# Stores of tiles that ScalarE evicts in the input projection: begun by ScalarE instead of SyncE

## The chip, the core and the metric

The kernel runs on one core of a Trainium2 chip. The time is the device time of one execution in microseconds, as the median of several runs. The core has TensorE (PE in the profile; its weight loads are PEld), VectorE (DVE), ScalarE (ACT), GpSimd (POOL) and SyncE (SP). Each executes its own list of instructions in order. A DMA is an instruction on one of these lists too: its engine waits until the DMA's conditions hold, hands it over to the DMA engines, and goes on. In rows of the profile such instructions carry the name of the engine with a q (SPq, ACTq).

## The reference, cut to what matters

The reference is one inference step of a decoder layer with two kinds of heads on a common input projection: eight heads of attention with forget gates (FoX), and four heads of an mLSTM with a 128 x 128 matrix memory. It handles 2048 new tokens of one prompt and 8 new tokens of each of 8 sampled sequences, which have 8192 past tokens in a paged cache.

```python
z = jnp.einsum('bsd,dc->bsc', x, w_in)          # x: 2048 + 64 tokens of 1024; w_in: 1024 x 3600
fq, fk, fv = z[..., :512], z[..., 512:1024], z[..., 1024:1536]     # attention; fk and fv are outputs
qk_in = z[..., OFF_M_QK:OFF_M_V]                # causal convolution of width 4, silu -> mLSTM q, k
mv = z[..., OFF_M_V:OFF_M_I]
og = jax.nn.sigmoid(z[..., OFF_M_O:] + b_og)    # output gate of the mLSTM
...
mix = jnp.concatenate([fox_h, mn], axis=-1) @ w_o
x1 = _layer_norm(DN_ALPHA * x + mix, ln1_g, ln1_b)
hid = jnp.square(jax.nn.relu(x1 @ w1))
return _layer_norm(DN_ALPHA * x1 + hid @ w2, ln2_g, ln2_b)
```

Keys, values, forget values, the mLSTM's last states and the last inputs of the convolution are outputs as well.

## The kernel before, in words

**Stages.** The work runs in stages: the input projection (up to 988 us of the profile), with the mLSTM beside it; the prompt's attention (to about 1440 us); the output projection with the first norm (to about 1720 us); the MLP with the second norm (the rest). The attention of the sampled sequences over the gathered cache pages runs beside all of them except the prompt's attention. All products of the main stream are exact to f32 by three matmuls on split operands (`mm3`, L137 to L140: high by high, high by low, low by high); ACT makes the high parts (`split_hi`, L130), DVE the low parts (L133).

**Input projection** (`block_a`, L395). It goes through four blocks of 512 prompt tokens (the first has the 64 sampled tokens besides). For each block the columns of w_in are taken in groups of 256: `wload` (L212) has SP load them (tile wra, L220), ACT and DVE split them. In this order the block makes

- mLSTM v, tokens on partitions (`natural`, L399): for each token tile 24 matmuls into a PSUM tile pm, which ACT copies into the SBUF tile st (`stage`, L412, copy L414); st is stored to the scratch dv (L420);
- mLSTM q and k, channels on partitions: ACT copies pm to qi (L447), DVE does the convolution, ACT the tanh (L457), DVE the last factor; stored to the scratch dqk (L459);
- the last rows of the convolution, stored to the outputs conv_sample and conv_prompt (L474, L482);
- the output gate, finished by DVE and stored to dog (L492);
- attention q: ACT scales pm into qst (L513), stored to dq (L514);
- attention k and v, again by copies of L414, stored to the outputs (L527, L532), from which later stages load them.

The PSUM tile pm has four buffers, the SBUF tile st four, wra two.

**mLSTM** (`m_block`, L575). It goes through 16 chunks of 128 tokens, one after another, each in several steps. A chunk loads its q and k (L586, from dqk), v (L589, from dv), two rows of gate values spread over all partitions (Wm, L591, from dM; qa, L593, from dar) and the output gate (og, L637, from dog). ACT takes the exponentials (L596, L598), PE multiplies (L604, L611, L621, L622, L629), ACT scales the result (hh, L573). Then `norm_out` (L544) norms it on DVE and POOL (up to L557), PE transposes it (L561), ACT copies it out of PSUM (ot, L563), and it is stored to the scratch dmix (L564). The tiles qk, Wm, qa, og and ot have one buffer each: the load of the next chunk waits for the last use in this one. `m_sample` (L650) does the same for the sampled sequences, with the state matrices of L707.

**Attention of the sampled sequences** (`sample_attention`, L1184). POOL gathers pages of keys (kraw, L1314) and of values (vt, L1401), two buffers each; DVE transposes the keys (L1316), PE makes the scores (L1327), DVE adds the forget sums (L1334) from tiles which SP loads (L1311); a softmax follows (L1361, L1371), then PE multiplies by the values (L1406).

**Order.** The side streams are cut into steps (`yield`). `tick` (L109) starts a step of the mLSTM for every 2.8 us of planned main-stream products and a step of the sampled attention for every 7.5 us (L21 to L24). From this order of the program a scheduler, which runs when the program is built (L1463), makes the lists of the five engines: it moves instructions against each other where their data permit it, by its own estimate of times. The lists are then fixed.

**Stores before the change.** All stores and loads of the input projection are begun by SP, which takes them in the order of its list. A store on SP waits there until the engine that makes the tile is done with it, and whatever stands behind it in SP's list waits as well. Only L1139 in the MLP has ACT begin loads (tile y).

**Semaphores of the DMAs.** The DMAs that SP and ACT begin take eight semaphores in turn, in the order in which the scheduler places them. Before a DMA is begun, the one before it on the same semaphore must have landed; where this isn't known already from an earlier wait, the list has a wait for it.

Of the kernel before, what the change touches and what calls it, by code (L numbers as in the profile page):

```python
# [19 lines left out]
# microseconds of the main stream's products per step of a side stream  # L20
# [32 lines left out]
def body(ctx, tc, I, O, stages):  # L53
# [3 lines left out]
    # ------------------------------------------------------------------ constants  # L57
# [25 lines left out]
    # pools of the sampled tokens' attention, which runs beside all phases, and of the mLSTM  # L83
# [6 lines left out]
    sqk = []                                         # new k of the sampled tokens  # L90
# [4 lines left out]
    gm = pm.tile([128, 16, 8], F32, name="gm")      # g = i - b and m, tokens on partitions  # L95
# [6 lines left out]
    def beside(gen):  # L102
        """one step of a side stream, whose instructions queue behind the main stream's latest"""
        with ExitStack() as es:
            for i in last.values():
                es.enter_context(tc.issue_after(i.ins))
            return next(gen, 0)

    def tick(us):  # L109
        """keeps the side streams in step with the main one"""  # L110
        macc[0] += us
        while macc[1] and macc[0] > PACE_M:
            macc[0] -= PACE_M
            if beside(macc[1][0]) == 0:
                macc[1].pop(0)
        if not macc[1]:
            macc[0] = 0.0
        acc[0] += us
        while acc[1] is not None and acc[0] > acc[2]:
            acc[0] -= acc[2]  # L120
            if beside(acc[1]) == 0:
                acc[1] = None
# [33 lines left out]
    # ------------------------------------------------------------------ phase A: input projection  # L156
# [16 lines left out]
    # conv weights transposed: [128 ch, 8 groups, 5] with the factor 1/2 of silu(c) = c/2 (1 + tanh(c/2))  # L173
# [38 lines left out]
    def wload(cols):  # L212
        """columns of w_in, [(first, number), ...], in their two parts, for each of the 8 row tiles"""
# [33 lines left out]
    def load_x(bi, tiles):  # L247
        """the block's x with channels on partitions, in two parts; column tiles of two token tiles"""
# [18 lines left out]
    def xcol(bi, t):  # L267
        """column tile and columns of a token tile"""
        blk, pre, off = geom(bi)
        o = off[t]  # L270
        i = int(o >= pre + 256)
        o -= i * (pre + 256)
        return xT[bi][i], slice(o, o + tok_n(t))

    def gate_stream(bi):
# [4 lines left out]
        def gates(z, lg, shape, bb):  # L280
# [16 lines left out]
            # log1p(e) = ln(u) + (e - (u - 1)) / u  # L297
# [21 lines left out]
        def rowset(cols, base, n_el, np_, sample):  # L319
# [32 lines left out]
            # M = m - b (kept in lr), ar = m0 - M, g = i - b  # L352
# [28 lines left out]
            # back to tokens on partitions: g, m  # L381
# [13 lines left out]
    def block_a(bi):  # L395
# [21 lines left out]
        for i in range(2):  # L417
            def sink(t, m, ps, i=i):
                r = tok_r(t)
                SY.dma_start(dv[r:r + m, i * 256:(i + 1) * 256], stage(ps[:, :256], m, 256))  # L420
                if i == 1:
                    V.tensor_copy((gats if t == 16 else gat[:, t])[:, 0:16], ps[:, 256:272])
            natural(sink, (C_V + i * 256, 256), *([(C_FF, 8), (C_I, 8)] if i == 1 else []),
                    hook=None if i else lambda n: load_x(bi, blk[n + 2:n + 3]))
# [3 lines left out]
        # mLSTM q/k, channels on partitions, causal convolution along the free axis  # L428
# [37 lines left out]
        if pre:  # L466
            # conv state of the sampled sequences
# [6 lines left out]
            SY.dma_start(O["conv_sample"].rearrange("l b j c -> (l b j) c"), cs_n)  # L474
        if bi == 3:
# [6 lines left out]
            SY.dma_start(O["conv_prompt"].rearrange("l b j c -> (l b j) c"), ch_n)  # L482
# [12 lines left out]
        # attention q, scaled, channels on partitions; that of the sampled tokens as [channel % 32, sequence, channel // 32, t]  # L495
        for j in range(4):
# [17 lines left out]
            SY.dma_start(dq[j, :, t0:t0 + 512], st)  # L514
            if pre and j % 2 == 1:
                SY.dma_start(dqb[0, :, :, j // 2 * 64:j // 2 * 64 + 64].rearrange("b p c -> p b c"), qr.rearrange("p b i t -> p b (i t)"))
        for i in range(2):
            def sink(t, m, ps, i=i):
# [8 lines left out]
                SY.dma_start(d, st)  # L527
            natural(sink, (512 + i * 256, 256))
        for i in range(2):
            def sink(t, m, ps, i=i):  # L530
                d = v_out(t)[:, i * 256:(i + 1) * 256]
                SY.dma_start(d, stage(ps, m, 256))  # L532
# [5 lines left out]
    # ------------------------------------------------------------------ phase M: mLSTM  # L538
# [5 lines left out]
    def norm_out(hh, np_, og, tok0):  # L544
        """per-head layer norm, output gate, transposed into the mix scratch"""
# [18 lines left out]
        SY.dma_start(dmv[:, 4:8, tok0:tok0 + np_], ot[:, :, :np_])  # L564

    def h_out(pn, h0, den, np_, hh):
        """h = num / max(|nq|, exp(-m)) for the pair of heads in pn"""
# [82 lines left out]
    def m_sample():  # L650
        # the sampled sequences: 8 new tokens each on their own state
# [19 lines left out]
        # keys of the sequence itself only: s >= 8 b  # L671
        for h in range(4):
            G.affine_select(Wv[:, h], Wv[:, h], pattern=[[-8, 8], [0, 8]], compare_op=OP.is_ge, fill=0.0, base=0, channel_multiplier=1)
        # bm[s, b] = 1 where token s belongs to sequence b
# [4 lines left out]
        # w_key[s] = W[s, last token of s's sequence]  # L679
# [25 lines left out]
        for h in range(4):  # L705
# [6 lines left out]
            # inter part, transposed [e, (b t)], and its normaliser row  # L712
# [5 lines left out]
            # n . q for all pairs (token, sequence), own sequence picked below  # L718
# [20 lines left out]
            # state update  # L739
# [47 lines left out]
    # ------------------------------------------------------------------ phase B: prompt attention  # L787
    def phase_b():
# [8 lines left out]
        def bank():  # L797
            """a bank of PSUM, every third time that of the sampled tokens' attention, which rests"""
# [13 lines left out]
        def twice(src, t):  # L812
            """a head's columns of token tiles, side by side with themselves"""
# [5 lines left out]
        def forget_values(z, a, n):  # L819
            """forget sums and values of the keys a .. a + n - 1"""  # L820
# [4 lines left out]
        def keys(z, g):  # L825
            """[k_hi; k_lo] of 512 keys, channels on partitions"""
# [14 lines left out]
        def queries(z, g):  # L841
            """[q_hi; q_hi] and [q_lo; q_lo] of two query tiles"""
# [10 lines left out]
        def scores(z, g):  # L853
            """scores of two query tiles against their causal keys, with -L of the keys and the row maximum"""
# [34 lines left out]
        def values(z, g, sc):  # L889
            """exponentials, row sums, weighted values [channels, queries]"""  # L890
# [8 lines left out]
            # P^T in chunks of four key tiles; even and odd key tiles add up in two column halves  # L899
# [31 lines left out]
        def finish(z, half):  # L931
            """1 / row sums as a row, spread over the head's partitions"""
# [44 lines left out]
    # ------------------------------------------------------------------ phase O: output projection, first norm  # L977
# [6 lines left out]
    def raw():  # L984
        """a slot of the ring for weights on their way in"""
        return pcw.tile([128, 1024], F32, name="wr", bufs=4)

    def landing(n=128):
        """a slot of the ring for activations on their way in"""
# [46 lines left out]
    # ------------------------------------------------------------------ phase C: MLP, second norm  # L1036
    def phase_c():
# [5 lines left out]
        def piece(src):  # L1043
            """a 4 KB piece of a weight matrix in its two parts"""
# [14 lines left out]
        def sampled():  # L1059
            """output projection and first norm of the sampled tokens"""  # L1060
# [22 lines left out]
        def load(ci):  # L1083
            """the block's tokens with channels on partitions, in two parts"""
# [99 lines left out]
def sample_attention(tc, I, O, ps_, pps, cst, ident, sqk, dnl, dR, dmix, dqb):  # L1184
    """FoX attention of the sampled tokens over the gathered pages."""
    nc = tc.nc
    V, A, G, T, SY = nc.vector, nc.scalar, nc.gpsimd, nc.tensor, nc.sync
    # ---- indices
# [7 lines left out]
    V.tensor_scalar(io[:, 0:1], pi, 31, None, op0=OP.bitwise_and)             # p % 32  # L1196
    V.tensor_scalar(io[:, 1:2], pi, 5, None, op0=OP.logical_shift_right)      # p // 32
    V.tensor_scalar(io[:, 2:3], pi, 7, None, op0=OP.bitwise_and)              # q
    V.tensor_scalar(io[:, 3:4], io[:, 0:1], 3, None, op0=OP.logical_shift_right)  # pg within a head's 32 rows
    fo = ps_.tile([128, 8], F32, name="fo")  # L1200
    V.tensor_copy(fo[:, 0:4], io[:, 0:4])
    V.scalar_tensor_tensor(fo[:, 4:5], fo[:, 0:1], 4.0, fo[:, 1:2], op0=OP.mult, op1=OP.add)  # (p%32)*4 + p//32
    V.scalar_tensor_tensor(fo[:, 5:6], fo[:, 1:2], 8.0, fo[:, 2:3], op0=OP.mult, op1=OP.add)  # (p//32)*8 + q
    for f in range(2):
        V.tensor_scalar(fo[:, 6 + f:7 + f], fo[:, 0:1], 2.0, float(f), op0=OP.mult, op1=OP.add)   # (p%32)*2 + half
# [5 lines left out]
    # V tile (unit u, page group g): partition (k, t) holds tokens 4 t .. 4 t + 3 of page 16 g + 4 u + k  # L1211
# [12 lines left out]
    # ---- reverse cumulated forget values of the past, written to the dR scratch as [b, h, page, (t%4, t//4)]  # L1224
    tri = ps_.tile([128, 128], F32, name="tri")
    V.memset(tri, 1.0)
    # lhsT[p', p]: p' > p in the same half
# [26 lines left out]
    # ---- new keys of the own sequence: additive bias [(h4, pg, q), t]  # L1254
# [8 lines left out]
    # ---- new k with channels on partitions, [sequence, channel % 32, channel // 32, t]  # L1263
# [7 lines left out]
    # ---- row (h4, q) selectors for the row sums: sel[k=(h4,pg,q), hg, m=(pair, h4, q)]  # L1271
# [32 lines left out]
    def k_step(b, kt, m):  # L1304
        """a quarter of the key tiles kt, kt + 1, channels on partitions"""
# [12 lines left out]
    def qk_step(b, kt):  # L1318
        """scores of the key tiles kt, kt + 1"""
# [18 lines left out]
    def softmax(b):  # L1338
# [11 lines left out]
        # maximum over a row's four page groups, through 32x32 transposes  # L1350
# [30 lines left out]
    def weights(b, u):  # L1381
        """transposed weights of a unit: [(k, t), hg, t%4, pg, h4, q]"""
# [10 lines left out]
    def pv_step(b, kt, f):  # L1393
        """rows (t % 2, hg, h4, q) against the values of the four heads of hg"""
# [72 lines left out]
```

## Time and profile before

| | |
|---|---|
| time, median of 3 runs | 3497.39 us (3494.44 to 3507.39) |
| span of the profiled execution | 3492.4 us |
| instructions | 59522 |
| clock of TensorE granted, mean over the span | 0.985 |
| DMA traffic | 663.15 MB in 446040 packets, 190 GB/s |
| moved by DMAs that ACT begins (queue q10) | 8.65 MB |

The profile is that of one execution, and its span runs from the first to the last instruction; the page gives no other time for it. An engine counts as busy while it computes; instructions that begin a DMA do not count. A row of waits says which engine stood, at which line, and what ended the wait, with the total, the number of cases and the longest one. In a row of the timeline the number in square brackets is the engine's idle time just before the instruction, with the instruction that ended it. A busy TensorE is not one at its peak, since matmuls overlap.

### The profile page before, as it was taken

Reading aid. Unit: us, or ns where it says so; the run is one execution under the profiler, and the core shown is the slowest. Engines: PE = TensorE matmul, PEld = TensorE weight load, DVE = VectorE, ACT = ScalarE, POOL = GpSimd, SP = SyncE. Lnnn points to the kernel's source line nnn. Section 1 sums busy time; section 2 is a strip of 40 time slices with the busy share of each in tenths; the row PEclk is TensorE's granted clock in tenths of the full one; section 3 lists DMA queues with packets and bytes.
Section 4 is the critical chain, followed back from the end, with each engine's and each line's share of the span. In section 5 each row is a group of like instructions: output and inputs, shape, how many; then the busy total and the mean of one; then the engine's idle time right before and its main releaser. Section 6 shows DMA issues by size and latency. Waiting matters only on the chain.

```text
span 3492.4 us, 59522 instructions
## 1 busy us (share of the span) xinstructions
PE 3354.9 (96%) x22428; PEld 2670.1 (76%) x22428; DVE 2178.9 (62%) x5302; ACT 1366.6 (39%) x2818; POOL 897.4 (26%) x942
## 2 busy tenths in 40 slices
PE   8899899999989999999899999999999999999998
PEld 8898778888866666667567677677677777898887
DVE  6747747657558787655556567666666544654555
ACT  3333323334358888512324243332233333443332
POOL 1013213231322222265332324223324111100000
PEclk9999999999999999999899999999999999999999
DMA  6557777775853232586776767768768555442221
GB/s 198 167 167 223 223 220 237 245 246 174 275 163 86 75 81 57 172 275 215 273 250 197 266 214 262 258 200 271 253 218 296 192 164 176 148 154 73 85 85 64
DMA packets 446040, 663.15 MB, mean 190 GB/s; under 512 B 84604, under 2 KB 333760, under 8 KB 444856
## 3 DMA queue, kind: packets, MB, share of 16 engines
q1 hardware_dynamic: 369064, 380.13, 36.1%
q0 software_dynamic: 74304, 270.57, 22.5%
q10 hardware_dynamic: 2384, 8.65, 0.7%
q8 instruction: 176, 2.88, 0.3%
q14 instruction: 112, 0.92, 0.1%
HBM read 598.01 MB, written 61.22 MB: 189 GB/s over the span
## 4 chain that ended last, share of the span: by engine, by line
PE 69%; DMA 15%; DVE 6%; issue 5%; POOL 3%; ACT 1%; SPq 0%; POOLq 0%; DVEq 0%; ACTq 0%
PE py L138 7%; PE py L140 6%; PE py L139 6%; PE ph L138 6%; PE ph L139 6%; PE ph L140 6%; DMA kraw<-cache_k,idxK 4%; PE po L919 4%; DMA vt<-cache_v,idxV 4%; PE pt L910 4%; PE pm L138 4%; PE pm L139 3%; PE pm L140 3%; PE sO L1406 3%; PE pS L871 2%
## 5 line engine op out<-in xcount | busy, mean ns | idle before, releaser
L1150 DVE TENSOR_TENSOR y<-y,py 128x512 f32<-128x512 f32 (+1 forms) x476 | 319.3, 680 | 251.1 <-PE py L140 246.9
L138 PE MATMUL ph<-x1h,wh 128*128 128x512 f32 (+1 forms) x1280 | 455.5, 356 | 2.4 <-ACT wh L130 2.4
L130 ACT ACTIVATE wh<-wr 128x1024 fp32r<-128x1024 f32 x264 | 273.4, 1057 | 466.0 <-PE py L140 264.0
L139 PE MATMUL ph<-x1l,wh 128*128 128x512 f32 (+1 forms) x1280 | 454.7, 355 | 0.0
L140 PE MATMUL ph<-x1h,wl 128*128 128x512 f32 (+1 forms) x1280 | 453.7, 355 | 0.2 <-DVE wl L133 0.2
L1401 POOL DMA_INDIRECT vt<-cache_v,idxV x256 | 257.9, 1007 | 736.1 <-PE sO L1406 701.2
L1316 DVE STREAM_TRANSPOSE kT<-kraw 128x512 f32<-128x512 f32 x512 | 328.3, 684 | 179.8 <-DMA kraw<-cache_k,idxK 178.4
L138 PE MATMUL py<-wh,hh 128*128 128x512 f32 (+1 forms) x1088 | 431.6, 399 | 1.5 <-DVE y L1148 0.8
L139 PE MATMUL py<-wl,hh 128*128 128x512 f32 (+1 forms) x1088 | 429.6, 395 | 0.7 <-DVE wl L133 0.7
L140 PE MATMUL py<-wh,hl 128*128 128x512 f32 (+1 forms) x1088 | 429.1, 395 | 0.0
L1314 POOL DMA_INDIRECT kraw<-cache_k,idxK x256 | 280.9, 1097 | 571.3 <-DVE kT L1316 439.0
L133 DVE TENSOR_TENSOR wl<-wr,wh 128x1024 fp32r<-128x1024 f32 x264 | 333.2, 1269 | 91.4 <-PE ph L140 25.7
L138 PE MATMUL pm<-whi,xh 128*128 128x256 f32 (+2 forms) x1088 | 320.3, 294 | 7.5 <-DVE st L489 4.8
L139 PE MATMUL pm<-wlo,xh 128*128 128x256 f32 (+2 forms) x1088 | 315.7, 290 | 0.0
L140 PE MATMUL pm<-whi,xl 128*128 128x256 f32 (+2 forms) x1088 | 315.4, 290 | 0.0
L138 PEld LDWEIGHTS ph<-x1h,wh 128*128 128x128 f32 x1280 | 240.9, 188 | 46.5 <-issue 11.1
L140 PEld LDWEIGHTS ph<-x1h,wl 128*128 128x128 f32 x1280 | 240.7, 188 | 42.8 <-issue 11.1
L139 PEld LDWEIGHTS ph<-x1l,wh 128*128 128x128 f32 x1280 | 240.6, 188 | 40.4 <-issue 8.6
L138 PEld LDWEIGHTS py<-wh,hh 128*128 128x128 f32 (+1 forms) x1088 | 201.3, 185 | 62.7 <-issue 18.1
L140 PEld LDWEIGHTS py<-wh,hl 128*128 128x128 f32 (+1 forms) x1088 | 201.3, 185 | 55.5 <-issue 9.9
L139 PEld LDWEIGHTS py<-wl,hh 128*128 128x128 f32 (+1 forms) x1088 | 201.5, 185 | 48.5 <-issue 8.6
L138 PE MATMUL pm<-xh,whi 128*128 128x256 f32 (+1 forms) x768 | 224.7, 293 | 0.8 <-ACT qi L447 0.8
(359 smaller groups left out, 6875.1 us busy)
## 6 DMA issues: line engine op xcount, KB each, us to landing
wr<-w SPq DMA_DIRECT2D x256, 512.0 KB
wra<-w_in SPq DMA_DIRECT2D x112, 512.0 KB
xn<-x_prompt SPq DMA_DIRECT2D x32, 512.0 KB
Rb<-dR SPq DMA_DIRECT2D x128, 128.0 KB
dqk<-th SPq DMA_DIRECT2D x32, 256.0 KB
qk<-dqk SPq DMA_DIRECT2D x16, 512.0 KB
qn<-dq SPq DMA_DIRECT2D x128, 64.0 KB
wr<-w_o SPq DMA_DIRECT2D x16, 512.0 KB
```

The costliest lines, as they stand in the source:

```text
L130: last["ACT"] = A.activation(dst, src, AF.Copy, scale=scale)
L133: r = (eng or V).tensor_tensor(dst, src, hi.bitcast(F32), op=OP.subtract)
L138: T.matmul(ps, wh, xh, start=first, stop=False)
L139: T.matmul(ps, wh, xl, start=False, stop=False)
L140: last["PE"] = T.matmul(ps, wl, xh, start=False, stop=stop)
L910: T.transpose(pt[:, k], sc[i][0][k0 // 4][:, k * 128:(k + 1) * 128], ident)
L919: last["PE"] = T.matmul(po[c:c + 64, q0:], z["vn"][:, k], PT[:, k - k0, q0:], start=(k < 2), stop=(k >= nk - 2), skip_group_check=True)
L1150: V.tensor_tensor(y, y, ps, op=OP.add)
L1314: G.indirect_dma_start(out=kraw, out_offset=None, in_=ck, in_offset=IO(ap=idxK[:, b, kt + k, f:f + 1], axis=0))
L1316: V.transpose(z["kT"][:, k, 2 * f + i].rearrange("p b c -> p (b c)"), kraw[:, i * 512:(i + 1) * 512])
L1401: G.indirect_dma_start(out=vt.rearrange("p f c -> p (f c)"), out_offset=None, in_=cv, in_offset=IO(ap=idxV[:, b, pg * 4 + u, f:f + 1], axi ...
L1406: T.matmul(po[r:r + 32], z["PT"][:, hg, 2 * f + g, pg].rearrange("p h q -> p (h q)"), vt[:, g, hg * 256:(hg + 1) * 256], start=(kt == 0 an ...
```

## The change

Seven calls of `dma_start` go from SyncE (`SY`) to ScalarE (`A`). In each of them ScalarE makes the tile that is stored. The tiles, their buffers and the regions written stay as they are. The stores of tiles that DVE finishes (L459 to dqk, L492 to dog) stay on SyncE, as do all loads. The new file also lacks the comments and docstrings of the old one, with the line numbers kept.

```diff
         for i in range(2):
             def sink(t, m, ps, i=i):
                 r = tok_r(t)
-                SY.dma_start(dv[r:r + m, i * 256:(i + 1) * 256], stage(ps[:, :256], m, 256))
+                A.dma_start(dv[r:r + m, i * 256:(i + 1) * 256], stage(ps[:, :256], m, 256))
...
-            SY.dma_start(O["conv_sample"].rearrange("l b j c -> (l b j) c"), cs_n)
+            A.dma_start(O["conv_sample"].rearrange("l b j c -> (l b j) c"), cs_n)
...
-            SY.dma_start(O["conv_prompt"].rearrange("l b j c -> (l b j) c"), ch_n)
+            A.dma_start(O["conv_prompt"].rearrange("l b j c -> (l b j) c"), ch_n)
...
                 A.activation(st[:, i * 256:i * 256 + 256], ps[:, w - 256:], AF.Copy, scale=0.125)
-            SY.dma_start(dq[j, :, t0:t0 + 512], st)
+            A.dma_start(dq[j, :, t0:t0 + 512], st)
...
                 else:
                     st = stage(ps, m, 256)
-                SY.dma_start(d, st)
+                A.dma_start(d, st)
...
                 d = v_out(t)[:, i * 256:(i + 1) * 256]
-                SY.dma_start(d, stage(ps, m, 256))
+                A.dma_start(d, stage(ps, m, 256))
...
         A.copy(ot[:, :, :np_], po[:, :, :np_])
-        SY.dma_start(dmv[:, 4:8, tok0:tok0 + np_], ot[:, :, :np_])
+        A.dma_start(dmv[:, 4:8, tok0:tok0 + np_], ot[:, :, :np_])
```

In order these are L420, L474, L482, L514, L527, L532 and L564; together 137 DMAs.

## The prediction

> **What bounds the kernel now.** First the head of the page, then the busy time of each engine in stretches: the part in which the seven changed lines run (25 to 988 us), the hand-over to the prompt attention (988 to 1004 us) and the output projection (1440 to 1720 us). The columns are length, then busy us and instructions of PE, PEld, DVE, ACT, POOL, granted clock, share of the DMA engines, GB/s.
>
> ```profile
> span 3492.4 us, 59522 instructions
> PE 3354.9 (96%) x22428; PEld 2670.1 (76%) x22428; DVE 2178.9 (62%) x5302; ACT 1366.6 (39%) x2818; POOL 897.4 (26%) x942
> ...
> 25.00:988.00 963.00, 905.72 (x7600) 829.61 (x7599) 605.33 (x1674) 319.61 (x699) 229.94 (x237) 0.98 0.69 213
> ...
> 988.00:1004.00 16.00, 6.76 (x38) 5.20 (x37) 6.97 (x29) 4.79 (x12) 5.24 (x9) 0.78 0.76 205
> ...
> 1440.00:1720.00 280.00, 258.53 (x1485) 185.15 (x1482) 152.45 (x323) 69.81 (x101) 153.35 (x123) 0.94 0.79 263
> ```
>
> TensorE sets the time: in the changed part it is busy for 905.72 of 963 us, one matmul in 905.72 / 7600 = 0.119 us. What a change that removes no matmul can win there is the 57.3 us in which PE stands, and a little clock (0.98 granted). ACT is busy for a third of it (319.61 us). So the next question is what PE stands for, read from the waits of PE (total us, times, longest), first between 18 and 988 us, then, last row, between 1440 and 1720 us.
>
> ```profile
> PE mm L561 <- POOL hh L557: 9.4, 6, 3.6
> PE mn L629 <- ACT hh L573: 4.8, 4, 2.3
> ...
> PE sT L1371 <- ACT Sn L1361: 4.6, 2, 4.3
> PE sQ L1327 <- DVE kT L1316: 4.3, 3, 3.6
> PE mm L604 <- DMA qk<-dqk: 3.9, 2, 2.8
> PE mm L715 <- DMA C<-state_C: 3.5, 3, 2.0
> ...
> PE sO L1406 <- DMA vt<-cache_v,idxV: 14.3, 8, 5.2
> ```
>
> No row names a load of w_in, and only two name a load that SP begins (qk, C: 7.4 us). The rest belongs to the side streams: steps of the mLSTM (L561, L629) and of the sampled attention (L1371, L1327) which stand at a fixed place in PE's program and are reached before their data is there. Now the queue that loses the stores: SP's own waits up to 1010 us.
>
> ```profile
> SPq L532 <- ACT st L414: 67.8, 28, 6.8
> SPq L527 <- ACT st L414: 64.6, 25, 6.2
> ...
> SPq L420 <- ACT st L414: 51.1, 20, 6.8
> ...
> SPq L591 <- PE mn L622: 25.7, 9, 7.9
> SPq L514 <- ACT qst L513: 25.0, 8, 8.5
> ...
> SPq L564 <- ACT ot L563: 6.6, 5, 2.6
> ```
>
> The moved stores (all but L591 here) hold SP for 67.8 + 64.6 + 51.1 + 25.0 + 6.6 = 215 us, always for a copy that ACT hasn't made yet. That is a large number on an engine that computes nothing; it counts only where a load behind it comes late for PE.
>
> **The change part by part.** In the built program 137 DMAs go from SP's list (1406 entries to 1269) to ACT's (2437 to 2574), one table load on ACT disappears, and no other instruction is added or lost. But the scheduler deals the order anew: the lists of PE, DVE and ACT differ from about 140 to 1100 us of today's time, again from 1520 to 1700 us (output projection), and nowhere else.
>
> *SP without the stores.* The 215 us of waits go. What sits behind them: w_in loads, for which PE waits nowhere; and the mLSTM's loads, for which it waits 7.4 us. The longest of these (2.8) follows the dqk store of L459, which DVE feeds and which stays on SP. What is late next is those loads' own conditions (L591 waits for PE's L622). Bounds 0 and -7.4 us; I take **-1**, nearer to nothing.
>
> *The new order in the mLSTM.* From the fifth to the twelfth of 16 chunks its steps stand some 100 matmuls (12 us) later in PE's list. A constant lag changes no wait; the distance between a step and the one it needs does. Between the last L629 of a chunk and its L561, the distance has a median of 11 matmuls before and about 20 after: 9 x 0.119 = 1.1 us more time for the norm that L561 waits for. The six waits (9.4 us, mean 1.6) shrink by about that much where they are met again: **-5**, bounds 0 and -9.4.
>
> *The new order in the sampled attention.* Its L1327 steps stand up to 29 matmuls earlier in eight cases, typically 20, that is 2.4 us, and wait for the keys (4.3 us in three cases now). Bounds 0 and 8 x 2.4 = +19; I take **+2**, half of today's wait, since most steps have slack. In the output projection L1406 and L1327 stand on average 16 matmuls earlier, at 258.53 / 1485 = 0.174 us each 2.8 us; there the values' gathers arrive last already (14.3 us in 8 cases). The gathers set the pace, so the loss is paid about once: **+2**, bounds 0 and 45 x 0.174 = +8 (45 being the largest shift).
>
> *137 issues on ACT.* What one costs SP today, and what ACT's own loads at L1139 cost (min/median/max ns); then ACT in time around such loads, start and length in us.
>
> ```profile
> L527 SPq DMA_DIRECT2D k_prompt<-st x32: 332/350/1881, 185.6 to 957.1; - x32
> ...
> L1139 ACTq DMA_DIRECT2D y<-dx x17: 326/443/721, 1711.9 to 3080.3; - x17
> ...
> 2644.83 0.37 ACTq L1139 DMA_DIRECT2D y<-dx  x1
> 2645.30 0.60 ACT L1122 ACTIVATE hq<-ph 128x512 f32<-128x512 f32 x1 [2.33 <-PE py L140]
> ...
> 3071.66 1.06 ACT L130 ACTIVATE wh<-wr 128x1024 fp32r<-128x1024 f32 x1 [1.45 <-DMA wr<-w]
> 3071.68 1.36 ACTq L1139 DMA_DIRECT2D y<-dx  x3
> 3073.08 0.41 ACT L1122 ACTIVATE hq<-ph 128x288 f32<-128x288 f32 x1 [0.37 <-issue]
> ...
> 3078.88 0.45 ACT L130 ACTIVATE hh<-hq 128x288 fp32r<-128x288 f32 x1
> 3080.32 0.50 ACTq L1139 DMA_DIRECT2D y<-dx  x1
> 3080.92 0.41 ACT L1122 ACTIVATE hq<-ph 128x288 f32<-128x288 f32 x1 [1.59 <-PE ph L140]
> ```
>
> An issue runs beside an activation already started (3071.66), and the next one begins only behind it (3071.68 + 1.36 = 3073.04, next at 3073.08). A moved store waits for the copy right before it, so nothing covers it on ACT: about 0.4 us each, 137 x 0.4 = 55 us of ACT. ACT has two thirds of the part free: 643 us.
>
> ```profile
> L414 ACT COPY st<-pm 128x256 f32<-128x256 f32 (+1 forms) x97 | 35.8, 370 | 148.3 <-PE pm L140 128.2 <-issue 14.5 <-remote 3.8
> ```
>
> Before its 97 copies ACT stands 148.3 us, 128.2 of them because PE hasn't finished the product: 1.5 us in front of each. The cover is this idle time and the four PSUM tiles of tag pm (a product is 24 matmuls, 2.9 us, so PE feels ACT only when it is three products, 8.6 us, late). Uncovered is about a third of the issues (ACT busy 33%): 137 x 0.33 x 0.36 = 16 us of delay on ACT, the upper bound; below is 0, and I take **+1**, as PE waits for ACT only at a few steps (L629, L1371).
>
> [...]
>
> *Waits for semaphores.* All these DMAs share eight semaphores in turn; a DMA waits until the one before it on its semaphore has landed. In the new program 89 of the 137 stores carry such a wait, 59 of them for a DMA of SP. That wait is new on ACT, and behind it stand evictions, exponentials and weight splits. The last three rows above show one on ACT: free at 3079.33, issue at 3080.32, 1.0 us, one case in 17. At that rate it is 8 us for 137 stores, under the cover: **0**, bounds 0 and +8. *The table load:* ACT alone, **0**.
>
> Sum: 3492.4 - 1 - 5 + 2 + 2 + 1 = 3491.4 us of span. The page gives only the span of the profiled execution; the median of the runs shown (3497.39) lies 5.0 above it, so **3496.4 us**. The bounds add up to -17 and +51, but not all at once.
>
> A stall is worth more than its length when the clock falls with it. Two stretches in front of and behind a stall, twice, and the stalls:
>
> ```profile
> 317.00:321.00 4.00, 2.11 (x20) 1.62 (x22) 3.39 (x8) 3.95 (x10) 2.43 (x6) 1.00 0.22 78
> 321.00:324.50 3.50, 3.50 (x34) 1.67 (x27) 3.50 (x8) 0.49 (x2) 2.92 (x3) 0.52 0.75 250
> 735.00:743.00 8.00, 4.40 (x40) 3.89 (x33) 3.15 (x5) 4.49 (x10) 5.32 (x5) 1.00 0.30 88
> 743.00:747.00 4.00, 4.00 (x36) 4.00 (x36) 0.00 (x0) 0.96 (x2) 1.01 (x1) 1.00 0.90 214
> ...
> 319.08 0.71 PE L629 MATMUL mn<-va,kw 128*128 128x129 f32 x4 [1.53 <-ACT hh L573]
> ...
> 742.84 0.66 PE L561 MATMUL mm<-ident,hh 128*128 128x128 f32 x4 [3.60 <-POOL hh L557]
> ```
>
> Behind a wait of 1.53 us the clock is 0.52 for 3.5 us, which costs 3.5 x 0.48 = 1.7 us; behind one of 3.60 us it stays 1.00. So each of the waits above may cost 1.7 us more, or not: three of them either way, +-5 us, which I put into the range. [...]
>
> **The rivals.** (1) *Faster, 3472 us:* SP's 215 us are what makes the mLSTM's data late. For it: ACT itself stands for such a load, and the load is long.
>
> ```profile
> ACT Wm L596 <- DMA Wm<-dM: 45.7, 14, 5.0
> ...
> 677.17 6.37 DMA Wm<-dM
> ```
>
> If loads that leave earlier take away the five waits of the mLSTM and of its loads (9.4 + 4.8 + 3.9 + 3.5 = 21.6 us, less the -6 counted) and five clock drops (8.5 us), the sum falls by 24. Against it: L591 waits for PE's own L622 (25.7 us), not only for stores.
>
> (2) *Slower, 3525 us:* ACT held by SP. Fourteen stores have the load of L591 or L593 in front of them on their semaphore. Such a load waits up to 7.9 us for PE and takes 6.4 to land: 14.3 us, 5.7 beyond the cover of 8.6. Five such cases make +28. It decides once ACT is over 8.6 us late. Against it: by the times of before, the DMA in front has landed at 128 of the 137 stores before the copy ends.
>
> (3) *Slower, 3516 us:* PE meets the gathers earlier than counted: +19 in the attention's steps instead of +2, and a clock drop or two.
>
> That the change does not take place is excluded by the instruction lists.
>
> **How the numbers follow.** My forecast, 3496.4 with 3480 to 3514 as its own range, has 0.74; rival 1 0.11, rival 2 0.09, rival 3 0.06. 0.5% is 17.5 us, about what a measurement of this kernel can tell from no change. Faster by more: 0.11; slower by more: 0.09 + 0.06 = 0.15; within: 0.74. The range of 8 in 10 reaches a little into rivals 1 and 3: 3474 to 3518.
>
> **What would show it.** Right: SP's rows for st and qst gone; ACT's DMA rows near 0.35 to 0.5 us, its stretch 25 to 988 still idle by half; the wait of L561 down to some 4 us, that of L1406 behind 1440 us up by 2; the hand-over to the attention near 1004 us, give or take 8. Wrong: waits of PE's L138 for ACT's copies, or ACT standing at a store for a DMA (rival 2); PE idle under 35 us in the part (rival 1).

## The result and the profile after

The changed kernel takes 3510.41 us, median of 7 runs (3504.34 to 3522.91), beside 3497.39 us: a ratio of 1.0040, with a 95% interval of 1.0023 to 1.0057. Set against the kernel before once more, in a later set of runs, it was at 1.0020 [1.0005, 1.0035] (last experiment). So it is slower by some 0.3%, 10 us. The forecast was 3496.4 us, 1 us less than before.

The head of the page after:

```profile
span 3508.7 us, 59451 instructions
...
PE 3359.6 (96%) x22428; PEld 2671.4 (76%) x22428; DVE 2178.6 (62%) x5302; ACT 1367.7 (39%) x2818; POOL 900.8 (26%) x942
```

The span is 16.3 us longer, the same matmuls keep PE busy 4.7 us longer. Where that lies, the hand-over to the prompt's attention tells: its first L871 starts at 1003.8 us before and at 1019.7 after. From there on the same matmul comes 16 to 20 us later in the prompt's attention, 15 to 28 in the output projection, 11 to 18 in the MLP, and 16 at the end. So on balance the loss is in the input projection. The stretch up to the hand-over, before and then after (columns: length, then busy us and instructions of PE, PEld, DVE, ACT, POOL, granted clock, DMA share, GB/s):

```profile
0.00:1003.80 1003.80, 927.37 (x7726) 848.87 (x7726) 628.51 (x1753) 334.94 (x726) 241.74 (x260) 0.98 0.70 214
```

```profile
0.00:1019.70 1019.70, 938.14 (x7726) 854.51 (x7726) 629.33 (x1753) 335.18 (x726) 242.74 (x260) 0.97 0.69 211
```

The same 7726 matmuls. PE's gaps, length less busy time, go from 76.4 to 81.6 us. The busy time itself goes up by 10.8 us, and the clock shows why. Where it is granted at half, at 839.94 to 843.35 us of the kernel before, the 128x256 matmuls of the main stream start 0.213 us apart, right behind it at full clock 0.120 us. The clock records of the trace have 14 windows of 3.41 us at half clock before and 21 after (counted to the end of the windows in which the hand-over falls). Half of each is taken as lost, an estimate: 23.9 and 35.8 us. By the spacing of these matmuls it is 1 - 0.120 / 0.213 = 0.44 of each, 21 and 31 us.

What PE waits for between 18 and 988 us of the changed kernel:

```profile
PE sQ L1327 <- DVE kT L1316: 9.8, 3, 4.8
PE mg L386 <- DVE gm L388: 7.9, 2, 4.6
PE mm L561 <- POOL hh L557: 7.8, 4, 3.0
PE mn L629 <- ACT hh L573: 6.7, 3, 3.1
PE mm L604 <- DMA qk<-dqk: 4.9, 2, 2.7
...
PE pm L138 <- DVE st L489: 3.5, 1, 3.5
PE pm L138 <- DVE xl L133: 3.1, 3, 1.4
PE sT L1371 <- ACT Sn L1361: 2.8, 1, 2.8
```

At the top stand two others than before: the sampled attention's scores (L1327, 4.3 before) and the small transposes that turn the mLSTM's gate rows back to tokens on partitions (L386, 2.5 before: each waits until DVE's L388 has copied the one before it out of the only PSUM buffer). L561, which should have gained most, went from 9.4 to 7.8. But the changed kernel is less far in its work at 988 us; counted up to the hand-over (before, then after) L561 gained 3.0 us:

```profile
PE mm L561 <- POOL hh L557: 13.9, 7, 4.5
```

```profile
PE mm L561 <- POOL hh L557: 10.9, 5, 3.1
```

None of the rows is a wait of a main product for one of ACT's L414 copies.

On SP the rows for st and qst are gone. What SP waits for up to 1030 us now:

```profile
SPq L220 <- DVE wlo L133: 129.1, 48, 10.2
SPq L637 <- POOL hh L557: 56.2, 10, 11.1
SPq L1311 <- DVE mxs L1334: 43.2, 15, 11.5
```

The w_in loads (L220, 57.3 us before) arrive at SP earlier and stand there until their buffer is free: SP's freed time turned into other waiting. And the issues on ACT, for two of the seven lines (ns, min/median/max):

```profile
L527 ACTq DMA_DIRECT2D k_prompt<-st x32: 338/339/627, 185.4 to 973.5; - x32
```

```profile
L532 ACTq DMA_DIRECT2D v_prompt<-st x32: 338/338/352, 220.4 to 1004.8; - x32
```

### The profile page after: what moved, and what is told of

It reads as the page before. It is cut to its first block, busy times and chain, and to the rows that moved or that the text cites. A ratio compares the mean times of both kernels' runs of the same rounds, so it can differ in the third digit from the quotient of the medians.

```text
span 3508.7 us, 59451 instructions
## 1 busy us (share of the span) xinstructions
PE 3359.6 (96%) x22428; PEld 2671.4 (76%) x22428; DVE 2178.6 (62%) x5302; ACT 1367.7 (39%) x2818; POOL 900.8 (26%) x942
## 3 DMA queue, kind: packets, MB, share of 16 engines
q1 hardware_dynamic: 343438, 358.52, 34.1%
## 4 chain that ended last, share of the span: by engine, by line
PE 67%; DMA 16%; issue 7%; DVE 6%; POOL 3%; ACT 1%; SPq 0%; POOLq 0%; ACTq 0%; DVEq 0%
PE py L138 6%; PE py L140 6%; PE py L139 6%; PE ph L138 5%; PE ph L139 5%; PE ph L140 5%; DMA kraw<-cache_k,idxK 5%; DMA vt<-cache_v,idxV 4%; PE po L919 4%; PE pt L910 4%; PE pm L138 3%; PE pm L140 3%; PE pm L139 3%; PE sO L1406 3%; PE sQ L1327 2%
## 5 line engine op out<-in xcount | busy, mean ns | idle before, releaser
L138 PE MATMUL ph<-x1h,wh 128*128 128x512 f32 (+1 forms) x1280 | 455.7, 356 | 2.9 <-ACT wh L130 2.9
L138 PE MATMUL py<-wh,hh 128*128 128x512 f32 (+1 forms) x1088 | 430.7, 398 | 1.5 <-DVE y L1148 0.9
L138 PE MATMUL pm<-whi,xh 128*128 128x256 f32 (+2 forms) x1088 | 320.5, 295 | 7.2 <-DVE st L489 3.5
L138 PEld LDWEIGHTS ph<-x1h,wh 128*128 128x128 f32 x1280 | 241.0, 188 | 46.8 <-issue 11.5
L138 PEld LDWEIGHTS py<-wh,hh 128*128 128x128 f32 (+1 forms) x1088 | 200.7, 185 | 62.6 <-issue 17.7
L1406 PE MATMUL sO<-vt,PTs 128*32 128x256 f32 x2048 | 192.0, 399 | 38.3 <-DMA vt<-cache_v,idxV 37.3
```

The costliest lines, as they stand in the source:

```text
L138: T.matmul(ps, wh, xh, start=first, stop=False)
L1406: T.matmul(po[r:r + 32], z["PT"][:, hg, 2 * f + g, pg].rearrange("p h q -> p (h q)"), vt[:, g, hg * 256:(hg + 1) * 256], start=(kt == 0 an ...
```

## The experiments

The change does two things: ACT issues 137 stores, and the scheduler, given another program, deals the order anew. The first pairs take these apart. Orders are forced by edges without semaphores, with the lists of a built program (`ORDER`) in the kernel:

```diff
     with tile.TileContext(nc, schedule_with_timeline_sim=True) as tc:
         body(tc, I, O, "SBMOC")
+        follow(tc)   # each instruction behind the one before it in its engine's ORDER
```

The 137 stores are left out of ORDER where they are on the other engine than in the list's own kernel.

**ACT's issues in the old order** (the changed kernel and `follow` with the lists of before):

> All 137 stores are issued by ScalarE, as in the changed kernel, but every engine's other instructions are held (by order-only edges, no semaphore) to the order that they had in the kernel before. Theory O, the order: the 13 us come from where the scheduler put the side streams' steps in TensorE's list, so this is back at 3497 +-4, with the first L871 within 3 us of 1003.8. Rival I, the issue: the 137 issues of 0.4 us on ScalarE and their waits delay ScalarE's copies and exponentials, so this stays at 3507 to 3513, with L871 near 1019. Half and half would be 3503.

3498.06 us, 1.0015 [1.0006, 1.0024]; the time is as theory O has it, but the hand-over is at 1012.0 us, 8 us late, which it excludes. **SP's issues in the new order** (the kernel before and `follow` with the lists of the changed kernel):

> The mirror: all stores are issued by SyncE, as before, but every engine's other instructions are held to the order that they have in the changed kernel. Theory O: 3507 to 3513, as slow as the changed kernel, L871 near 1019. Rival I: 3497 +-4. If issue and order both matter, the two mirrors add up: what this gains over 3510 and what the first gains over 3510 sum to 13 us.

3501.98 us, 1.0029 [1.0014, 1.0044]. Some two thirds of the first loss, 1.0040, come without the change's own work, by order alone; a smaller part may be the issues'.

**Parts of the change, scheduler free.** Only L420, then all but L420:

```diff
-                SY.dma_start(dv[r:r + m, i * 256:(i + 1) * 256], stage(ps[:, :256], m, 256))
+                A.dma_start(dv[r:r + m, i * 256:(i + 1) * 256], stage(ps[:, :256], m, 256))
```

> Only the 34 stores of the mLSTM values (L420) move to ScalarE; the scheduler is free. TensorE's list then differs from the changed kernel's in 906 places of 19328, and from that of before in 4562. Theory O: nearly the changed kernel's time, 3506 to 3513. Rival I: a quarter of the issues, so a quarter of the loss, 3500 to 3502.

> 103 of the 137 stores move, all but those of L420; the scheduler is free. TensorE's list differs from that of before in 553 places of 19328, and from the changed kernel's in 4612. Theory O: 3497 +-4. Rival I: three quarters of the loss, 3506 to 3508.

3498.12 us, 1.0007 [0.9991, 1.0023], and 3508.58 us, 1.0032 [1.0020, 1.0044]: both against theory O as stated. The second alone is about what rival I says, the first isn't. The kernel nearer to the new order loses nothing, the one nearer to the old order as much as the whole change. Closeness of the lists tells nothing: 553 places out of 19328, with three quarters of the issues, suffice. The trace of the first says where its loss went: its hand-over is at 1021.8 us, as late as the changed kernel's, and the output projection, where its order is another one, wins part of it back: from the last L871 to the first L1094 it takes 234.9 us, and 242.0 before. The rest lies in the MLP, and can be chance: from the first L1094 to the end the 17 traces take 1805.6 to 1826.5 us.

**One side stream at a time**, on SP, by lists merged from the two:

> SyncE issues all stores, as before. The steps of the mLSTM and of its gates stand where the changed kernel has them among the main stream's instructions; those of the sampled tokens' attention stand where the kernel before has them. The mirror with the whole new order on SyncE was at 1.0029. Theory S, the attention steps (L1327 met 20 matmuls earlier, its waits on kT 9.3 us instead of 4.3 in phase A) carry the order's cost: this is at 0.999 to 1.001, 3491 to 3498. Rival M, the mLSTM and gate steps (L386's wait for gm 8.4 us instead of 2.5) carry it: 1.002 to 1.003, 3501 to 3505. Rival C, neither: any rearrangement costs about as much through the clock windows that it shifts: this and the next run are each at 1.001 to 1.003 and don't add up.

> The mirror of the run before: SyncE issues all stores, the steps of the sampled tokens' attention stand where the changed kernel has them, those of the mLSTM and its gates where the kernel before has them. Theory S: 1.002 to 1.003, 3501 to 3505, with some 9 us of waits of L1327 for kT in phase A. Rival M: 0.999 to 1.001. Rival C: 1.001 to 1.003 for both.

3538.81 us, 1.0141 [1.0126, 1.0155], and 3539.68 us, 1.0150 [1.0133, 1.0166]. All three theories missed by far. The hand-over, at 1033.9 and 1033.5 us, holds 30 of about 50 us. But the merged lists don't set the two streams apart cleanly: on DVE, 73 and 47 places at which before and after have the same line hold another one here, and where the attention moved, L1327 waits only 1.9 us for kT, not the 9 expected. So these runs price two further orders. That a stream set back alone clashes with the others is a likely reading, not shown.

**Twice the issues, old order**, each store in two halves of its partitions:

```diff
-                A.dma_start(dv[r:r + m, i * 256:(i + 1) * 256], stage(ps[:, :256], m, 256))
+                put(A, dv[r:r + m, i * 256:(i + 1) * 256], stage(ps[:, :256], m, 256))   # 2 DMAs
```

> As the first run (ScalarE issues the stores, all other instructions in the order of before), but each of the 137 stores is issued in two halves of its partitions, so 274 issues on ScalarE. The first run was at 1.0015 [1.0006, 1.0024]. Theory I, these 5 us are the cost of the issues: the second 137 cost as much again, 1.003, 3504. Rival N, the 5 us are not the issues' (the queue's shared semaphores, or chance): 1.001 to 1.002, 3498 to 3501.

3498.27 us, 1.0012 [0.9995, 1.0029]: rival N. 137 further issues show no cost; the interval leaves room for some 0.15%.

**Another order, nothing else**, from the kernel before:

```diff
-PACE_M = 2.8
+PACE_M = 2.85
```

> The kernel before, its stores on SyncE, with PACE_M 2.85 instead of 2.8: the mLSTM's steps are dealt out 2% sparser, nothing else is changed, and the scheduler rearranges TensorE's list in phase A. Theory C (any rearrangement of the side streams' steps costs some 0.2%, as it costs stalls and half-clock windows that the order of before happens to lack): 1.001 to 1.004. Rival: orders lie on both sides of that of before alike, 0.998 to 1.002, and the changed kernel's order is a bad one among them.

3495.31 us, 1.0002 [0.9986, 1.0019]. Not every rearrangement costs in the whole; but its hand-over too is late, 1019.6 us, with 81.3 us of gaps, and the output projection made up for a part of it (234.8 us, measured as above). The waits of PE up to 1030 us are other ones than in the changed kernel:

```profile
PE mm L561 <- POOL hh L557: 17.2, 8, 4.3
...
PE sQ L1327 <- DVE kT L1316: 3.4, 2, 3.1
```

So the stages had to be priced apart. The prompt's attention has one order in the lists concerned, and they can be joined there:

```diff
+ORDER: the changed kernel's lists up to matmul 9355 of TensorE, those of before behind it (and so on)
```

> SyncE issues all stores. Up to the middle of the prompt attention (matmul 9355 of 19328 in TensorE's list) every engine follows the changed kernel's order, behind it that of before: the input projection alone is rearranged. Theory T: the time follows the sum of TensorE's idle gaps, which the order fixes (before 123.8 us, changed 135.3, the whole new order on SyncE 137.1), and clock drops even out over runs. Of the 13 us that the whole order added, 7 lay before 1030 us: this has 84 to 86 us idle in the first 1030 us, 129 to 133 in all, and is at 1.0015 to 1.0025. Rival K: the extra half-clock windows of the input projection (37.5 us lost in it instead of 23.9) are the order's too and come in every run: 1.004 or more.

> The mirror: the order of before in the input projection, the changed kernel's from matmul 9355 on, so in the output projection (L1406 waits 25.5 us for vt there in the changed kernel, 18.6 before). Theory T: 5 us more idle than before, 128 to 131, 1.001 to 1.0015. Rival K: 1.000, as the changed kernel lost nothing behind 1030 us in its one profile.

> SyncE issues all stores; the order of before in the input projection, and from matmul 9355 on the order of the kernel that moved the stores of L420 alone, which had 21.9 us of gaps in the output projection where before has 26.8 (L1406 waits 16.8 us for vt instead of 18.6). Theory T: 3 to 6 us less idle than before, 118 to 121 in all, 0.998 to 0.999, 3484 to 3489: a version that beats both. Rival K: 1.000.

> The kernel before against itself, unchanged: what one set of 12 runs can tell, and what one profile can. Theory T: 1.000 +-0.0015; idle gaps within 3 us of the first profile's 123.8 us, while the time lost to half clock, 54.1 us in the first profile (23.9 before 1014 us), differs by 5 us and more. Rival K: the clock loss of the input projection repeats to 3 us.

| kernel (all on SP) | median us | ratio, 95% interval |
|---|---|---|
| new order in the input projection alone | 3509.00 | 1.0036 [1.0022, 1.0050] |
| new order behind matmul 9355 alone | 3492.67 | 0.9981 [0.9970, 0.9991] |
| order of "only L420" behind matmul 9355 | 3487.24 | 0.9973 [0.9960, 0.9987] |
| the kernel before again | 3495.63 | 0.9996 [0.9983, 1.0009] |

The new order of the input projection carries the loss; that of the output projection wins a little. Between theory T (gaps alone, 1.0015 to 1.0025) and rival K (the half clock comes with the order, 1.004), the first run is nearer to K, though its interval touches T; the clock of all its runs decides for K (below). The second lies outside of both theories, and the third won a little more than T put. The third beats both kernels. The kernel before again is the same within 0.2%, but two profiles of it differ by 5.3 us in the half clock of the whole span and by 6 us in PE's waits: that is what one profile can tell. Waits (18 to 988 us) and hand-over of the first, then the hand-over of the third and of the kernel before again:

```profile
PE mg L386 <- DVE gm L388: 9.7, 2, 6.3
PE sQ L1327 <- DVE kT L1316: 9.7, 3, 4.9
PE mm L561 <- POOL hh L557: 6.8, 5, 2.3
```

```profile
0.00:1022.20 1022.20, 937.61 (x7726) 853.77 (x7726) 628.91 (x1753) 334.89 (x726) 242.83 (x260) 0.97 0.69 210
```

```profile
0.00:1001.40 1001.40, 925.60 (x7727) 847.94 (x7727) 627.80 (x1753) 334.94 (x726) 243.89 (x260) 0.98 0.70 215
```

```profile
0.00:1005.30 1005.30, 928.04 (x7726) 849.99 (x7726) 628.18 (x1753) 335.70 (x726) 245.15 (x260) 0.97 0.70 214
```

Last, the suspected line put back, the best order with the change, and the change once more. For the first, 144 matmuls of L1327 and L1345 stand 5 to 34 main matmuls later in TensorE's ORDER:

> As the run with the new order in the input projection alone (1.0036 [1.0022, 1.005], 84.1 us of gaps before 1020 us where before has 78 to 79), but in TensorE's list the eight groups of L1327 and the one of L1345, 144 matmuls, stand again as many main-stream matmuls in as they did before, 5 to 34 later; nothing else is moved. Theory S, the attention steps met too early (L1327 waits 9.3 us for kT instead of 4.3) are the cause: gaps of 78 to 80 us, 1.000 to 1.0015, 3497 to 3502. Rival M, the mLSTM's and gates' steps are (L386 waits 8.4 us for gm instead of 2.5): 1.003 to 1.004, 3507 to 3511, gaps of 83 to 85 us.

> ScalarE issues all 137 stores, as in the changed kernel; the order of before in the input projection, and behind matmul 9355 the order that was worth 0.9973 [0.996, 0.9987] with SyncE. Theory I, ScalarE's issues cost some 0.13% at an unchanged order (1.0015 and 1.0012 measured): 0.998 to 0.9993, 3490 to 3494, faster than both kernels though it makes the change. Rival N, those 0.13% were chance: 0.9965 to 0.998.

> The changed kernel once more, beside the parts. If the parts add up (order of the input projection +0.36%, order of the output projection -0.19%, the issues on ScalarE +0.13%): 1.003, 3506 to 3508. If the issues cost more where they meet the new order: 1.004 and more.

3515.12 us, 1.0083 [1.0066, 1.0100]; 3480.08 us, 0.9982 [0.9965, 0.9998]; 3495.71 us, 1.0020 [1.0005, 1.0035]. The first is outside of both theories: L1327 no longer waits for kT, and others wait longer.

```profile
PE mm L561 <- POOL hh L557: 12.5, 5, 4.5
PE mn L629 <- ACT hh L573: 10.4, 5, 3.6
PE mg L386 <- DVE gm L388: 6.8, 3, 4.0
...
PE mm L611 <- DVE Wm L607: 4.9, 1, 4.9
PE mn L629 <- DVE wlo L133: 4.6, 1, 4.6
```

Only TensorE's list was changed there, and the lists of all engines may have to fit each other; so whether the attention's or the mLSTM's and gates' steps are to blame has no answer by moving one of them. That stays open; what is shown is the order of the input projection as a whole. The second run makes the very change and is faster than both kernels, since it keeps the old order in the input projection and takes the better one behind it; its interval covers both theory I and rival N. The parts add up within their intervals: +0.36% and -0.19% for the order, +0.12% for the issues (1.0015, 1.0012, and 0.9982 over 0.9973), together +0.29%, beside +0.40 and +0.20 measured. (The whole new order on SP had +0.29%, its two stages sum to +0.17%; what lies between them is within the intervals too.)

The traces side by side, up to the hand-over (gaps as above; lost = half of the time at half clock, the estimate above):

| order of the input projection | hand-over, us | gaps, us | lost at half clock, us |
|---|---|---|---|
| old, SP (before; again; two late orders) | 1003.8, 1005.3, 1009.6, 1001.4 | 76.4, 77.3, 81.6, 75.8 | 23.9, 27.3, 29.0, 23.9 |
| old, ACT (one issue; halves; late order) | 1012.0, 1012.7, 1006.6 | 78.4, 77.8, 79.6 | 32.4, 35.8, 23.9 |
| new, ACT (after; again) | 1019.7, 1027.3 | 81.6, 83.7 | 35.8, 44.4 |
| new, SP (whole; early alone) | 1022.7, 1022.2 | 85.0, 84.6 | 37.5, 37.5 |
| all but L420; PACE_M 2.85 | 1022.9, 1019.6 | 82.9, 81.3 | 39.3, 37.5 |
| only L420; L1327 put back | 1021.8, 1026.2 | 80.6, 89.8 | 41.0, 35.8 |
| one stream moved: mLSTM; attention | 1033.9, 1033.5 | 85.9, 89.5 | 44.4, 34.1 |

Length less gaps less loss is 899 to 904 us in every trace but the last (910): little else varies. With SP, the new order adds 17.4 us on the mean (1022.5 against 1005.0): 7.0 by gaps (84.8 against 77.8), 11.5 by half clock (37.5 against 26.0; 1.1 us too much together: the last windows reach beyond the hand-over, and half of each is more than the spacing of the matmuls gives). The medians have 12 of these 17 us; one profile is one execution, and the MLP alone varies by 21 us between the traces.

The half clock need not rest on single profiles: the granted clock of every run is on record, and (1 - clock) x span estimates the time lost in it, again at half of each stretch. With the new order in the input projection alone this is 64.0 us on the mean of 12 runs, beside 53.9 in 34 runs of the kernel before: 10.1 of the 12.3 us by which the mean span grew. With the whole new order on SP it is 9.1 of 12.0 us, in the changed kernel again 7.9 of 7.8. At 0.44 instead of half it is 8.8, 7.9 and 6.9 us. Most of the loss is clock.

## Why the prediction went wrong, point by point

**The clock, taken at nothing (+-5): the step that failed most.** The forecast let three stalls fall either way. The profiles show 11.5 us, one way, and the clocks of all runs 10.1. A half-clock window costs 1.5 us by the spacing of 0.213 instead of 0.120 us (1.7 at half of its 3.41), and put to the line with the longest gap in the window ahead, L1327 has 3 to 5 of them in five traces (four of the new order, one of only L420) and 0 to 2 in seven of the old one, L386 2 to 4 and 0 to 1. Their waits in the changed kernel are few and long (up to 4.8 and 4.6 us). That these two lines are the cause is not shown: all but L420 and PACE_M 2.85 lost as much, 39.3 and 37.5 us, with one or no window at each of them.

**The sampled attention, +2.** L1327 waits 9.8 us instead of 4.3, +5.5, by the mechanism and within the bounds of the step (0 to +19); the chosen value was too near to nothing. With its clock windows this is what rival 3 described (PE meets its data earlier, plus a clock drop or two, 3516 us). It had a chance of 0.06 and came nearest, with smaller stalls and more drops than it named.

**The mLSTM, -5.** The mechanism held, the size less so: up to the hand-over L561 has 13.9 to 16.5 us in four traces of the old order on SP and 10.3 to 12.6 in four of the new one, 3.6 less on the mean; L629 and L604 change by 0.4 and 0.2. What failed is what the term left out: the gates, a part of the same stream whose distances changed too, were not looked at, and L386 went from 2.2 to 7.9 us on the same means (2.5 to 7.9 in the two kernels). On balance a loss of some 3 us where a gain of 5 was put.

**The output projection, +2.** Wrong in sign, if small: the new order there alone is worth -0.19% [-0.30, -0.09], 6.6 us. The sign that the forecast named did come, between 1440 and 1740 us of the changed kernel (14.3 us before), and misled: a longer wait at this line isn't a longer stage.

```profile
PE sO L1406 <- DMA vt<-cache_v,idxV: 19.6, 10, 5.5
```

**SP's freed time, -1, and the issues on ACT, +1.** Right in the gaps, up to the hand-over. One reading ahead of it was incomplete: a third row of PE names a load that SP begins (L262 for x_prompt, 1.6 us). At the old order the gaps are the same with ACT as with SP to within the spread (77.8 to 79.6, and 75.8 to 81.6), and 274 issues cost no more than 137. The ratios leave +0.12%, 4 us, where the two terms sum to nothing. The profiles have 30.7 against 26.0 us of half clock, but the clocks of all runs don't bear that out (54.5 against 53.1 us with one issue, 53.3 against 52.2 with halves); what makes the 4 us is not shown. The issues themselves are short: L527 and L532 have medians of 0.34 us in the rows above.

**The semaphores, 0.** Right for PE, as far as its waits show. In the changed kernel up to 1030 us, ACT does stand until stores have landed whose semaphore or buffer its next step needs; none of it comes through to L138, so rival 2 didn't come.

```profile
ACT qst L513 <- DMA dq<-qst: 6.5, 2, 4.1
...
ACT qi L447 <- DMA dmix<-ot: 2.7, 1, 2.7
ACT whi L130 <- DMA k_prompt<-st: 2.4, 1, 2.4
```

Of the signs named, that for rival 1 stayed out, and so did rival 2's waits of L138 for ACT's copies; its other sign, ACT standing for the landing of a store, came in the small as shown. Rival 1's sum also misread its rows: it speaks of five waits, and the four rows hold 15. The hand-over near 1004 +-8 did not hold, by 8 us, and that was the sign that an order had gone wrong.

## What to carry to other kernels

Where a scheduler deals the lists, an edit is two changes, the edit and the new deal; here the second was the larger, and the two can be measured apart by forcing one program's order on the other's instructions. Price a shifted step by the longest wait that it makes as well, clock included, and not by the sum of waits alone; and list the waits of every stream that shares the shifted engine. When the deal is the cost, take the order of the better kernel stage by stage: the change with the old order in one stage and another in the next beat both.

## What the runs showed of the hardware

In 17 traces every change of TensorE's clock lies on a grid of 3.413 us, to 0.002 of a window. What the clock did next went with the share of a window in which PE stood. The windows of these traces that lie between 25 and 3480 us, counted:

| PE idle in a window | windows | next window at half clock |
|---|---|---|
| at full clock, under 40% | 16172 | 16 |
| 40 to 50% | 160 | 18 |
| 50 to 60% | 101 | 68 |
| over 60% | 221 | 221 |
| at half clock, under 20% | 354 | 33 |
| at half clock, over 20% | 183 | 183 |

So at full clock half a window of standing, 1.7 us, was often enough, and 60% of one, 2.05 us, was enough each time.

Of the 16 exceptions in the first row, 14 hold matmuls of L715, with 8 columns each (128x8, 256 ns at the median), up to 16 in a window. With their time counted as idle, 11 of the windows in that row come out over 60%, and all 11 are followed by half clock; 33 come out at 50 to 60%, with the other 3. So for the clock these matmuls seem to count as idle time, though the profile has PE busy.

A wait in the changed kernel, L1327 at 295.8 us, in windows of that grid:

```profile
292.42:295.84 3.42, 3.38 (x29) 3.17 (x27) 0.34 (x1) 0.00 (x0) 0.00 (x0) 1.00 1.09 344
295.84:299.25 3.41, 0.00 (x0) 0.00 (x0) 1.70 (x6) 2.28 (x5) 1.18 (x1) 1.00 0.68 253
299.25:302.67 3.42, 2.05 (x18) 0.96 (x20) 3.41 (x7) 2.02 (x2) 1.18 (x1) 0.50 0.39 138
302.67:306.08 3.41, 3.41 (x16) 2.54 (x12) 3.35 (x12) 0.63 (x1) 0.00 (x0) 0.50 0.63 163
306.08:309.49 3.41, 3.41 (x33) 2.80 (x33) 2.45 (x13) 0.68 (x1) 0.00 (x0) 1.00 0.52 150
```

An empty window, then one at half clock which is 40% idle (2.05 of 3.42 busy), so that the next is at half clock too: one wait of 4.8 us costs two windows. It also solves the pair of stalls on which the forecast's clock term stood, in the kernel before:

```profile
317.70:321.11 3.41, 1.67 (x17) 1.38 (x21) 3.41 (x8) 3.36 (x7) 2.54 (x6) 1.00 0.10 39
321.11:324.53 3.42, 3.42 (x34) 1.59 (x25) 3.42 (x8) 0.38 (x2) 2.81 (x3) 0.50 0.77 255
737.54:740.95 3.41, 1.70 (x15) 1.49 (x13) 1.90 (x2) 2.95 (x5) 3.30 (x4) 1.00 0.23 78
740.95:744.37 3.42, 1.53 (x13) 1.53 (x14) 1.25 (x4) 0.58 (x1) 2.89 (x2) 1.00 0.70 171
744.37:747.78 3.41, 3.41 (x31) 3.41 (x30) 0.17 (x1) 0.37 (x1) 0.00 (x0) 1.00 0.93 238
```

The wait of 1.53 us, but for its start, and a short one behind it lie in one window and leave it 51% idle: half clock. That of 3.60 us is cut in two by the grid, 50 and 55% idle, in the band where both outcomes occur, and nothing follows. The grid does not begin with the kernel: its first line lies 0.26 us behind the first instruction in the trace of before (317.70 - 93 x 3.4133), 2.29 us in that of after (292.42 - 85 x 3.4133). So the same stalls can lie otherwise on it in another execution; the same order lost 35.8 and 44.4 us in two.
